# Where the decay tables of a chunked scan are made: inside the forward scan, or ahead of it during the attention and parked in DRAM

## The chip, the cores and the metric

The kernel runs on one core of one Trainium2 chip. The metric is the device time of one execution in microseconds. The kernel before took 2136.37 us, the median of three runs (2135.49 to 2142.13).

## The reference, cut to what matters

Two layers of a hybrid encoder run on 1040 tokens (16 learned ones and 1024) of 1024 channels. Each layer is a norm, one wide projection that is split among four mixers (pooling, a 2-D Fourier transform, a bidirectional scan, attention with eight query heads), their gates, and an output projection with a residual sum. The change is in the scan mixer (SSD):

```python
dt = softplus(dt_raw.reshape(b, n, 2, SSD_HEADS) + dt_bias)
a = -exp(a_log)
...
cs = cumsum(dt * a, axis=-1)                      # within a chunk
seg = cs[..., :, None] - cs[..., None, :]
lmat = exp(where(lower, seg, -inf))
cb = einsum("bclgn,bcsgn->bcgls", cc, bc)
y_diag = einsum("bcgrls,bcsgrp->bclgrp", cb[:, :, :, None] * lmat, x * dt)
decay_to_end = exp(cs[..., -1:] - cs)
chunk_states = einsum("bclgn,bcgrl,bclgrp->bcgrpn", bc, decay_to_end, x * dt)
... # states carried from chunk to chunk
y_off = einsum("bclgn,bcgrpn,bcgrl->bclgrp", cc, prev, exp(cs))
y = y_fwd + y_bwd + d_skip * x
```

For each chunk and head, `lmat` times `dt` is a 104x104 table that depends on `dt` alone and not on the chunk's B, C and x. The forward and the backward direction use two halves of it (a lower and an upper triangle), so the kernel makes both in one table.

## The kernel before, in words

Data lie with channels on partitions. A layer is written as a set of Python generators, each of which issues a few instructions per step. `weave` interleaves several generators in proportion to given step counts, `run` runs them out, and a scheduler then arranges each engine's instructions. So the order around the change is set by step counts (`FN`, `LS`, `PS`, `TT`), by buffer counts (`NBIG` 30 tiles `big`, `NBB` 5 tiles `bb`, `NPF` tiles `pf`) and by the rings of PSUM tiles. Each engine runs its own instructions strictly in that order.

A layer goes through these stages:

- Projections, `mm3`: each product is three matmuls of split operands (L132 to L134). `split` makes the operands on ScalarE (L128) and VectorE (L129).
- Attention in four head pairs, t = 0 to 3. `att_q` and `att_max` prepare the next pair: the row maxima come from scores L626 and the reduction L627 on VectorE, 54 per pair and layer. `att_main` makes the scores again (L655, L656), exponentials on ScalarE (L658) into tiles `pf`, sums of them into `acc` (L666, L668; on GpSimd, six of sixteen on VectorE), the weighted values on PE (L678), and the division. Woven with it runs `fill`, the other projections, which are spilled to DRAM in the order of the string `FO`: U and P (pooling), F (Fourier gate), D (`spill_dt` and `ssd_dt`), C (convolution), R, Z. L621 is a copy within SBUF on GpSimd's DMA queue.
- `ssd_dt` makes from `dt` the running sums `csd`, the decays `ecd` and the token table `tkd`, and writes them to DRAM.
- The Fourier stages (L525 copies a product from PSUM), `ssd_load` (SiLU of the convolved inputs, L306 and the lines behind it on ScalarE), and `ssd_bwd`, the states of the backward direction.
- `ssd_fwd`, the forward scan, in 10 chunks of 104 tokens. `prepare(q)` loads both `csd` rows of a chunk, broadcast over partitions (`rf`, `rb`, two of the five tiles `bb`), and builds the table: the products of C and B in PSUM are masked into `cfb` (L880, L881); for each of eight heads VectorE adds a gap and takes a minimum (L883), ScalarE takes the exponential (L884); ScalarE scales one masked product (L887), VectorE adds the other (L888); GpSimd multiplies the two (L889). `finish(q)` loads `ecd` into a tile `big`, multiplies the contributions of the states from PSUM by it (L900, L903), adds them on GpSimd (L908), carries the state on in `ssd_state` (VectorE L808, PE L811, GpSimd L817, VectorE L818), multiplies the table with x on PE (L914), and adds D times x (L917).
- Woven into the scan, the output projection of the attention. Its group with `pool=True` copies a sum from PSUM on ScalarE (L349), adds the residual on GpSimd (L350) and stores it (L353); it loads into tiles `sms` (L338), of which there are four.

The code of the functions that the change touches:

## Time and profile before

| what | value |
|---|---|
| median of three runs | 2136.37 us |
| profiled execution, time | 2144.23 us |
| its span and mean granted TensorE clock | 2142.5 us, 0.969 |
| TensorE busy | 2007.5 us, 94% |
| VectorE, ScalarE, GpSimd busy | 65%, 47%, 22% |
| forward scans | about 925 to 1050 us and 1981 to 2100 us |
| head pairs of the attention | about 150 to 640 us and, in layer 1, 1205 to 1695 us |

Busy shares are averages over stages that differ, so the windows of single stages carry the argument. A row of a group gives line, engine, operation, output and inputs with their shapes, count, then busy us in all, mean ns of one, and the idle time just before with what ended it. A matmul's duration overlaps with its neighbours', so counts times durations of matmuls aren't added up; a stretch's busy time divided by its count is used for the pace.

### The profile page before, as it was taken

The page shows a single profiled execution, that of the slowest core. Times are in us where ns is not written, and L with a number is a line of the kernel's source. Part 1 is how long each engine was busy: PE and PEld are TensorE (multiplying, and loading weights), DVE is VectorE, ACT ScalarE, POOL GpSimd, SP SyncE. Part 2 cuts the span into 40 slices and gives each one's busy share as a digit, 9 for nine tenths or more (in the row PEclk, how much of TensorE's full clock was granted, in tenths as well). Part 3 has the DMA queues.
Part 4 walks back from the last instruction along what each step waited for, and adds up shares of the span by engine and source line. Part 5 has one row for each costly group of instructions (what it writes and reads, how often), then busy time and mean ns, then how long its engine had stood idle before and what let it go on. Part 6 is the DMA issues. An engine that isn't in the chain of part 4 may idle for free.

```text
span 2142.5 us, 33401 instructions
## 1 busy us (share of the span) xinstructions
PE 2007.5 (94%) x11880; PEld 1756.2 (82%) x11880; DVE 1398.6 (65%) x2785; ACT 1012.6 (47%) x2191; POOL 464.2 (22%) x465
## 2 busy tenths in 40 slices
PE   6999999999999898888889999999999998979888
PEld 5898988688899568877779988877888995878878
DVE  5575547767664455689795655476675635476996
ACT  5534344453542546356464344435534433463652
POOL 2012122031110210245230221221311103012550
PEclk9999999999999999999999999998999999988999
DMA  4322222123233477676643221212223344776666
GB/s 138 99 74 62 64 63 57 43 76 97 91 127 104 135 210 246 193 187 191 169 123 116 66 67 54 73 44 72 68 98 102 117 129 127 241 217 180 175 184 195
DMA packets 164605, 261.01 MB, mean 122 GB/s; under 512 B 20878, under 2 KB 113618, under 8 KB 164438
## 3 DMA queue, kind: packets, MB, share of 16 engines
q1 hardware_dynamic: 161782, 249.55, 38.7%
q0 software_dynamic: 2656, 9.33, 1.8%
q8 instruction: 93, 1.52, 0.3%
q14 instruction: 74, 0.61, 0.1%
HBM read 182.91 MB, written 71.67 MB: 119 GB/s over the span
## 4 chain that ended last, share of the span: by engine, by line
PE 68%; DVE 14%; DMA 9%; ACT 4%; issue 3%; POOL 2%; SPq 1%; DVEq 0%; POOLq 0%; ACTq 0%
PE psmm L132 11%; PE psmm L133 10%; PE psmm L134 10%; PE pspv L678 6%; PE psy L132 5%; PE psy L133 5%; PE psy L134 5%; PE psy L655 2%; PE psy L626 2%; PE psy L656 2%; DMA hd<-sms 2%; DVE bb L883 1%; PE pssc L655 1%; DMA big<-ecd 1%; PE pssc L626 1%
## 5 line engine op out<-in xcount | busy, mean ns | idle before, releaser
L132 PE MATMUL psmm<-big,wh 128*128 128x346 f32 (+2 forms) x1920 | 645.5, 337 | 42.0 <-DVE sms L352 19.2
L133 PE MATMUL psmm<-big,wh 128*128 128x346 f32 (+2 forms) x1920 | 633.8, 330 | 7.6 <-DVE big L129 4.7
L134 PE MATMUL psmm<-big,wl 128*128 128x346 f32 (+2 forms) x1920 | 628.2, 327 | 1.3 <-DVE wl L129 1.3
L132 PEld LDWEIGHTS psmm<-big,wh 128*128 128x128 f32 x1920 | 370.8, 193 | 88.0 <-issue 29.3
L133 PEld LDWEIGHTS psmm<-big,wh 128*128 128x128 f32 x1920 | 371.0, 193 | 17.8 <-DVE big L129 7.2
L134 PEld LDWEIGHTS psmm<-big,wl 128*128 128x128 f32 x1920 | 371.3, 193 | 4.5 <-DVE wl L129 2.4
L668 POOL TENSOR_TENSOR acc<-acc,pf 116x346 f32<-116x346 f32 (+5 forms) x216 | 222.9, 1044 | 701.2 <-ACT pf L658 557.4
L128 ACT CAST wh<-wr 128x512 fp32r<-128x512 f32 (+1 forms) x236 | 145.2, 616 | 268.6 <-PE psmm L133 205.8
L129 DVE TENSOR_TENSOR wl<-wr,wh 128x512 fp32r<-128x512 f32 x232 | 168.4, 730 | 126.6 <-ACT wh L128 125.2
L132 PE MATMUL psy<-big,wh 128*128 128x346 f32 (+2 forms) x672 | 221.8, 330 | 1.1 <-ACT big L128 0.6
L133 PE MATMUL psy<-big,wh 128*128 128x346 f32 (+2 forms) x672 | 217.7, 324 | 3.1 <-DVE big L188 2.0
L134 PE MATMUL psy<-big,wl 128*128 128x346 f32 (+2 forms) x672 | 216.8, 323 | 0.0
L678 PE MATMUL pspv<-pf,vt 116*64 116x346 f32 (+5 forms) x864 | 168.8, 469 | 0.0
L658 ACT ACTIVATE pf<-psy 116x346 f32<-116x346 f32 (+4 forms) x288 | 125.3, 457 | 87.0 <-PE psy L656 84.8
L668 DVE TENSOR_TENSOR acc<-acc,pf 116x346 f32<-116x346 f32 (+5 forms) x120 | 106.7, 889 | 71.5 <-ACT pf L658 51.0
L627 DVE TENSOR_REDUCE mx<-psy 116x1 f32<-116x346 f32 (+3 forms) x272 | 132.7, 511 | 18.5 <-PE psy L626 18.0
L132 PEld LDWEIGHTS psy<-big,wh 128*128 128x128 f32 x672 | 127.2, 189 | 13.3 <-issue 7.6
L133 PEld LDWEIGHTS psy<-big,wh 128*128 128x128 f32 x672 | 127.0, 189 | 6.9 <-DVE big L188 3.1
L134 PEld LDWEIGHTS psy<-big,wl 128*128 128x128 f32 x672 | 127.0, 189 | 0.8
L678 PEld LDWEIGHTS pspv<-pf,vt 116*64 116x64 f32 (+1 forms) x864 | 59.4, 137 | 62.5 <-issue 26.7
L655 PE MATMUL psy<-big,big 128*116 128x346 f32 (+4 forms) x288 | 96.2, 336 | 0.9 <-DVE mx L627 0.8
L627 DVE TENSOR_REDUCE mx<-pssc 128x1 f32<-128x346 f32 (+3 forms) x136 | 69.8, 513 | 41.7 <-PE pssc L626 40.0
(293 smaller groups left out, 3326.7 us busy)
## 6 DMA issues: line engine op xcount, KB each, us to landing
wr<-w SPq DMA_DIRECT2D x248, 256.0 KB
sms<-hd SPq DMA_DIRECT2D x112, 173.0 KB
hd<-sms SPq DMA_DIRECT2D x96, 173.0 KB
bb<-csd SPq DMA_DIRECT2D x40, 338.0 KB
md<-big SPq DMA_DIRECT2D x24, 520.0 KB
gd<-sms SPq DMA_DIRECT2D x64, 173.0 KB
big<-gd SPq DMA_DIRECT2D x16, 520.0 KB
big<-md SPq DMA_DIRECT2D x16, 520.0 KB
```

Of the source, the lines that this page charges most:

```text
L128: nc.scalar.copy(hi, src)
L129: nc.vector.tensor_tensor(lo, src, f(hi), op=ALU.subtract)
L132: nc.tensor.matmul(out_ps, ah, bh, start=start, stop=False)
L133: nc.tensor.matmul(out_ps, ah, bl, start=False, stop=False)
L134: nc.tensor.matmul(out_ps, al, bh, start=False, stop=stop)
L626: nc.tensor.matmul(p[:qn, :cw], s1[e][:, q0:q0 + qn], k1[:, c0:c0 + cw], start=True, stop=True)
L627: nc.vector.tensor_reduce(mx[:qn, q, e, ci:ci + 1], p[:qn, :cw], axis=AX.X, op=ALU.max)
L655: nc.tensor.matmul(p[:n, :cw], k1[:, k0:k0 + n], s1[e][:, cs], start=True, stop=False)
L656: nc.tensor.matmul(p[:n, :cw], k3[0:65, k0:k0 + n], q2[e][0:65, cs], start=False, stop=True)
L658: nc.scalar.activation(pf[:n, :cw], p[:n, :cw], AF.Exp, scale=0.125)
L668: eng.tensor_tensor(accs[c0, e][:n, :cw], accs[c0, e][:n, :cw], pf[:n, :cw], op=ALU.add)
L678: nc.tensor.matmul(hold["pv"][64 * e:64 * e + 64, :cw], s.vt[:n, k, v, :], pfs[e][:n, :cw], start=(k == 0), stop=(k == len(KTS) - 1))
```

## The change

The tables no longer wait for the chunk's B and C. A new generator, `ssd_tab`, makes decay times step size for each of ten chunks and each of two halves (four heads), in six steps per half, and stores the result in DRAM (`dec`). It is woven as one more stream into `att_main` of head pairs 1, 2 and 3, with 40, 44 and 40 steps. It uses a buffer `tb` and a token table `tk`, one of each. In the forward scan, `prepare` loads the finished table of a chunk (one load of 338 KB in the place of two) and multiplies it by the product of C and B from PSUM, two instructions on VectorE. The `ecd` load moves from `finish` to `prepare` and into a tile `bb`. `ssd_state` makes one product on VectorE and one on GpSimd where it made two of half the size. The projection of `dt` and `ssd_dt` go ahead of P and F in `FO`, and `ssd_dt` yields twice more in each of its five rounds. `NPF` goes from 14 to 12; the tiles `cfb` and `gap` are gone. The number of matmuls stays. ScalarE's table loads go from 61 to 57 in its order.

```diff
-    PB, KB, NPF, NACC = 2, 3, 14, 4
+    KB, NPF, NACC = 3, 12, 4
+    TT = (0, 40, 44, 40)
-    FO = 'UPFDCCCCCRCCCZ'
+    FO = 'UDPFCCCCCRCCCZ'
...
             nc.vector.tensor_scalar(t1[R], t1[R], -1.0, None, op0=ALU.mult)
+            yield
+            yield
             p = ps("xx")
...
+    def ssd_tab(l, s):
+        mf, mb = ct[:QC, C_MF:C_MF + QC], ct[:QC, C_MB:C_MB + QC]
+        s.dec = drp.tile([NQ, QC, 8 * QC], F32, name=nm("dec"))
+        for q in range(NQ):
+            tok = phase["p"].tile([QC, 152], F32, name=nm("tk"), tag="tk", bufs=1)
+            nc.sync.dma_start(tok[:, :144], s.tkd[q])
+            for a in range(2):
+                t = phase["p"].tile([QC, 3, 4, QC], F32, name=nm("tb"), tag="tb", bufs=1)
+                rf, rb, cf = t[:, 0], t[:, 1], t[:, 2]
+                col = lambda c, r: tok[:, c + 4 * a + r:c + 4 * a + r + 1]
+                nc.sync.dma_start(t[:, 0:2], s.csd[q, :, 4 * a:4 * a + 4].partition_broadcast(QC))
+                yield
+                for r in range(4):
+                    nc.scalar.activation(cf[:, r], mb, AF.Copy, scale=col(136, r))
+                if a == 0:
+                    nc.vector.tensor_tensor(tok[:, 144:152], tok[:, 32:40], tok[:, 0:8], op=ALU.subtract)
+                yield
+                for r in range(4):
+                    nc.vector.scalar_tensor_tensor(cf[:, r], mf, col(104, r), cf[:, r], op0=ALU.mult, op1=ALU.add)
+                gap = tok[:, 144 + 4 * a:148 + 4 * a].unsqueeze(2).broadcast_to([QC, 4, QC])
+                nc.gpsimd.tensor_tensor(rb, rb, gap, op=ALU.add)
+                yield
+                nc.vector.tensor_tensor(rf, rf, rb, op=ALU.min)
+                yield
+                for r in range(4):
+                    nc.scalar.activation(rf[:, r], rf[:, r], AF.Exp, bias=col(0, r))
+                yield
+                nc.gpsimd.tensor_tensor(rf, rf, cf, op=ALU.mult)
+                nc.gpsimd.dma_start(s.dec[q, :, 4 * a * QC:4 * a * QC + 4 * QC], rf)
+                yield
...
+        nc.vector.tensor_tensor(hv(xw), hv(x[:QC]), w.unsqueeze(3).broadcast_to([QC, 4, 2, 64]), op=ALU.mult)
...
+            nc.gpsimd.tensor_tensor(hv(new), hv(st), d.unsqueeze(3).broadcast_to([128, 4, 2, 64]), op=ALU.mult)
...
         def prepare(q):
-            rf, rb = vr(bb()[:QC]), vr(bb()[:QC])
-            nc.sync.dma_start(rf, s.csd[q, 0].partition_broadcast(QC))
-            nc.sync.dma_start(rb, s.csd[q, 1].partition_broadcast(QC))
+            rb, e = vr(bb()[:QC]), vr(bb())
+            nc.sync.dma_start(rb, s.dec[q].rearrange("s (r t) -> s r t", t=QC))
+            for a in range(2):
+                nc.sync.dma_start(e[64 * a:64 * a + 64].rearrange("p (i j) t -> p i j t", i=2), s.ecd[q, :, 4 * a:4 * a + 4].partition_broadcast(64))
...
-            nc.vector.tensor_tensor(cf, pcv, mf.unsqueeze(1).broadcast_to([QC, 2, QC]), op=ALU.mult)
-            nc.vector.tensor_tensor(cb, pcv, mb.unsqueeze(1).broadcast_to([QC, 2, QC]), op=ALU.mult)
-            for r in range(8):
-                nc.vector.scalar_tensor_tensor(rf[:, r], rb[:, r], s.gap[:, q, r:r + 1], rf[:, r], op0=ALU.add, op1=ALU.min)
-                nc.scalar.activation(rf[:, r], rf[:, r], AF.Exp, bias=tok[:, r:r + 1])
-            for r in range(8):
-                g = (r % 4) // 2
-                nc.scalar.activation(rb[:, r], cb[:, g], AF.Copy, scale=tok[:, 136 + r:137 + r])
-                nc.vector.scalar_tensor_tensor(rb[:, r], cf[:, g], tok[:, 104 + r:105 + r], rb[:, r], op0=ALU.mult, op1=ALU.add)
-            nc.gpsimd.tensor_tensor(rb, rb, rf, op=ALU.mult)
+            for a in range(2):
+                m = rb[:, 4 * a:4 * a + 4].rearrange("p (g i) t -> p g i t", g=2)
+                nc.vector.tensor_tensor(m, m, pcv, op=ALU.mult)
...
-        run(weave((att_main(l, s, t), LS + 3 * PC), (chain(*side), 20 + 3 * PC + 6), (islice(fill, n), n)))
+        run(weave((att_main(l, s, t), LS + 3 * PC), (chain(*side), 20 + 3 * PC + 6), (islice(fill, n), n), (islice(tab, TT[t]), TT[t] + 0.01)))
...
-        run(weave((islice(main, LS + 3 * PC - 1), LS + 3 * PC - 1), (chain(*side), PS), (chain(fill, islice(fill2, GP + FB[0])), WF * (n + GP + FB[0]))))
+        run(weave((islice(main, LS + 3 * PC - 1), LS + 3 * PC - 1), (chain(*side), PS), (chain(fill, islice(fill2, GP + FB[0])), WF * (n + GP + FB[0])), (tab, TT[3])))
```

In the kernel after, `ssd_tab` has these lines: loads L786 and L791, copies L794 and exponentials L806 on ScalarE, L799 and the minimum L803 on VectorE, the addition L801, the product L808 and the store L809 on GpSimd. The lines of before's attention stand one further there (L627 is L628, L668 is L669). In the scan the new products are L910; L900 and L903 have become L918 and L921.

What the order of each engine shows. On GpSimd, in head pair 1 of layer 0 before, there are only sums of exponentials:

```order
L666 TENSOR_TENSOR acc_1767<-pf_1734,pf_1760 116x346
L668 TENSOR_TENSOR acc_1767<-acc_1767,pf_1800 116x346
L668 TENSOR_TENSOR acc_1767<-acc_1767,pf_1853 116x346
L668 TENSOR_TENSOR acc_1769<-acc_1769,pf_1858 116x346
L668 TENSOR_TENSOR acc_1767<-acc_1767,pf_1880 116x346
L668 TENSOR_TENSOR acc_1767<-acc_1767,pf_1917 116x346
```

After, additions, products and stores of the tables stand between such sums; this is from head pair 2:

```order
L801 TENSOR_TENSOR tb_4517<-tb_4517,tk_4273 104x416
L669 TENSOR_TENSOR acc_2924<-acc_2924,pf_2994 116x348
L669 TENSOR_TENSOR acc_2926<-acc_2926,pf_2999 116x348
L669 TENSOR_TENSOR acc_2924<-acc_2924,pf_3025 116x348
L808 TENSOR_TENSOR tb_4517<-tb_4517 104x416
L809 DMA dec_2882<-tb_4517 104x416
L669 TENSOR_TENSOR acc_2924<-acc_2924,pf_3078 116x348
L801 TENSOR_TENSOR tb_4704<-tb_4704,tk_4702 104x416
```

A sum that stands behind an addition or a product of a table cannot start before it.

On VectorE, in the same stage before, row maxima of the next head pair are what stands between the sums and the splits:

```order
L627 TENSOR_REDUCE mx_2118<-pssc_2660 116x1
L627 TENSOR_REDUCE mx_2118<-psy_2663 116x1
L627 TENSOR_REDUCE mx_2118<-psy_2666 116x1
L668 TENSOR_TENSOR acc_2116<-acc_2116,pf_2677 116x346
L668 TENSOR_TENSOR acc_2116<-acc_2116,pf_2695 112x346
L627 TENSOR_REDUCE mx_2118<-psy_2708 116x1
L627 TENSOR_REDUCE mx_2118<-psy_2711 116x1
L627 TENSOR_REDUCE mx_2118<-pssc_2714 116x1
```

After, a minimum stands ahead of six maxima, and four scaled sums and the next minimum behind them:

```order
L803 TENSOR_TENSOR tb_3361<-tb_3361 104x416
L628 TENSOR_REDUCE mx_2183<-pssc_2430 116x1
L628 TENSOR_REDUCE mx_2183<-psy_2433 116x1
L628 TENSOR_REDUCE mx_2183<-psy_2436 116x1
L628 TENSOR_REDUCE mx_2183<-pssc_2458 116x1
L628 TENSOR_REDUCE mx_2183<-psy_2461 116x1
L628 TENSOR_REDUCE mx_2183<-psy_2464 116x1
L130 TENSOR_TENSOR wl_2514<-wr_2507,wh_2513 128x512
L633 TENSOR_REDUCE mneg_2822<-mx_2183 116x9
L799 SCALAR_TENSOR_TENSOR tb_3594<-ct,tk_3359,tb_3594 104x104 x4
L130 TENSOR_TENSOR wl_2756<-wr_2751,wh_2755 128x512
L803 TENSOR_TENSOR tb_3594<-tb_3594 104x416
```

In a layer the first minimum stands behind the 57th row maximum, the 19th behind the 148th, the last behind the 162nd.

On VectorE in the middle of the forward scan of layer 0, before:

```order
L883 SCALAR_TENSOR_TENSOR bb_9652<-bb_9653,gap_8183,bb_9652 104x104 x3
L880 TENSOR_TENSOR cfb_9496<-psy_9493,ct 104x208
L881 TENSOR_TENSOR cfb_9496<-psy_9493,ct 104x208
L883 SCALAR_TENSOR_TENSOR bb_9652<-bb_9653,gap_8183,bb_9652 104x104 x3
L888 SCALAR_TENSOR_TENSOR bb_9478<-cfb_9496,big_8184,bb_9478 104x104 x4
L883 SCALAR_TENSOR_TENSOR bb_9652<-bb_9653,gap_8183,bb_9652 104x104
L888 SCALAR_TENSOR_TENSOR bb_9478<-cfb_9496,big_8184,bb_9478 104x104 x4
L883 SCALAR_TENSOR_TENSOR bb_9652<-bb_9653,gap_8183,bb_9652 104x104
L808 TENSOR_TENSOR big_9491<-big_9491,big_8184 104x4x64 x2
L129 TENSOR_TENSOR wl_10100<-wr_10097,wh_10099 128x512
L900 TENSOR_TENSOR big_9557<-pssc_9560,big_9557 128x416
L903 TENSOR_TENSOR big_9557<-pspv_9566,big_9557 128x416
```

After, with a chunk's table loaded ready, two products by the PSUM tile take the place of these 18 instructions:

```order
L842 TENSOR_TENSOR big_10012<-big_10012,big_8576 104x512
L910 TENSOR_TENSOR bb_9997<-bb_9997,psxx_10014 104x416 x2
L130 TENSOR_TENSOR wl_10511<-wr_10508,wh_10510 128x512
L918 TENSOR_TENSOR bb_9840<-pssc_10057,bb_9840 128x416
L921 TENSOR_TENSOR bb_9840<-pspv_10063,bb_9840 128x416
```

The products of `ssd_state` (L808 before, L842 after) are one instruction, and L918 and L921 follow without the chain of small instructions ahead of them.

More of the change, by code (lines that the diff above doesn't have):

```diff
@@ L108, in chunk_tile @@
     def chunk_tile(tag, dt=F32):
-        return phase["p"].tile([128, 348], dt, name=nm(tag), tag=tag, bufs=NPF if tag == "pf" else PB)
+        return phase["p"].tile([128, 348], dt, name=nm(tag), tag=tag, bufs=NPF)
     def bb():
@@ L806, in ssd_state @@
         w = s.tok[q][:, 64 + 32 * i:72 + 32 * i].rearrange("p (a j) -> p j a", j=4)
-        for a in range(2):
-            nc.vector.tensor_tensor(hv(xw)[:, :, a], hv(x[:QC])[:, :, a], w[:, :, a].unsqueeze(2).broadcast_to([QC, 4, 64]), op=ALU.mult)
+        nc.vector.tensor_tensor(hv(xw), hv(x[:QC]), w.unsqueeze(3).broadcast_to([QC, 4, 2, 64]), op=ALU.mult)
         p = ps(tag)
@@ L815, in ssd_state @@
             d = s.decb[:, i, :, q].rearrange("p (a j) -> p j a", j=4)
-            for a in range(2):
-                nc.gpsimd.tensor_tensor(hv(new)[:, :, a], hv(st)[:, :, a], d[:, :, a].unsqueeze(2).broadcast_to([128, 4, 64]), op=ALU.mult)
+            nc.gpsimd.tensor_tensor(hv(new), hv(st), d.unsqueeze(3).broadcast_to([128, 4, 2, 64]), op=ALU.mult)
             nc.vector.tensor_tensor(new, new, p, op=ALU.add)
@@ L831, in ssd_load @@
         s.tok = []
-        s.gap = phase["p"].tile([QC, NQ, 8], F32, name=nm("gap"), tag="gap", bufs=1)
         for q0 in (0, 5):
@@ L836, in ssd_load @@
             s.tok += [t[:, i] for i in range(5)]
-            nc.vector.tensor_tensor(s.gap[:, q0:q0 + 5], t[:, :, 32:40], t[:, :, 0:8], op=ALU.subtract)
         s.xbc = [big() for _ in range(8)]
@@ L858, in ssd_fwd @@
         s.y = [s.xbc[j] for j in range(4)]
-        mf, mb = ct[:QC, C_MF:C_MF + QC], ct[:QC, C_MB:C_MB + QC]
         vr = lambda t: t[:, :8 * QC].rearrange("p (r t) -> p r t", t=QC)
@@ L876, in prepare @@
                 nc.tensor.matmul(pc[:QC, g * QC:(g + 1) * QC], s.xbc[4 + g][:, qs], s.xbc[6 + g][:, qs], start=True, stop=True)
-            cfb = phase["p"].tile([128, 4 * QC], F32, name=nm("cfb"), tag="cfb", bufs=1)[:QC].rearrange("p (g t) -> p g t", t=QC)
-            cf, cb = cfb[:, 0:2], cfb[:, 2:4]
-            pcv = pc[:QC, :2 * QC].rearrange("p (g t) -> p g t", t=QC)
-            nc.vector.tensor_tensor(cf, pcv, mf.unsqueeze(1).broadcast_to([QC, 2, QC]), op=ALU.mult)
-            nc.vector.tensor_tensor(cb, pcv, mb.unsqueeze(1).broadcast_to([QC, 2, QC]), op=ALU.mult)
-            for r in range(8):
-                nc.vector.scalar_tensor_tensor(rf[:, r], rb[:, r], s.gap[:, q, r:r + 1], rf[:, r], op0=ALU.add, op1=ALU.min)
-                nc.scalar.activation(rf[:, r], rf[:, r], AF.Exp, bias=tok[:, r:r + 1])
-            for r in range(8):
-                g = (r % 4) // 2
-                nc.scalar.activation(rb[:, r], cb[:, g], AF.Copy, scale=tok[:, 136 + r:137 + r])
-                nc.vector.scalar_tensor_tensor(rb[:, r], cf[:, g], tok[:, 104 + r:105 + r], rb[:, r], op0=ALU.mult, op1=ALU.add)
-            nc.gpsimd.tensor_tensor(rb, rb, rf, op=ALU.mult)
-            ready[q] = (xt, xw, bt, rb)
+            pcv = pc[:QC, :2 * QC].rearrange("p (g t) -> p g t", t=QC).unsqueeze(2).broadcast_to([QC, 2, 2, QC])
+            for a in range(2):
+                m = rb[:, 4 * a:4 * a + 4].rearrange("p (g i) t -> p g i t", g=2)
+                nc.vector.tensor_tensor(m, m, pcv, op=ALU.mult)
+            ready[q] = (xt, xw, bt, rb, e)
         def finish(q, st):
             qs = slice(q * QC, (q + 1) * QC)
-            xt, xw, bt, rb = ready.pop(q)
-            e = vr(big())
-            for a in range(2):
-                nc.sync.dma_start(e[64 * a:64 * a + 64].rearrange("p (i j) t -> p i j t", i=2), s.ecd[q, :, 4 * a:4 * a + 4].partition_broadcast(64))
+            xt, xw, bt, rb, e = ready.pop(q)
             if q < NQ - 1:
@@ L1034, in hybrid_trunk @@
         s.md["x"] = drp.tile([8, 128, L], F32, name=nm("md"))
-        kv = att_kv(l, s)
+        kv, tab = att_kv(l, s), ssd_tab(l, s)
         if l == 0:
```

1 line of the change is left out of this document (removed).

## The prediction

> **What bounds the kernel now.** I read the page first (busy time, chain), then the windows of busy time by stage, then groups, waits and timelines in the two stages touched. Line numbers are those of the kernel before unless "new" stands ahead.
>
> ```profile
> PE 2007.5 (94%) x11880; PEld 1756.2 (82%) x11880; DVE 1398.6 (65%) x2785; ACT 1012.6 (47%) x2191; POOL 464.2 (22%) x465
> PE 68%; DVE 14%; DMA 9%; ACT 4%; issue 3%; POOL 2%; SPq 1%; DVEq 0%; POOLq 0%; ACTq 0%
> ```
>
> TensorE bounds the program as a whole. That average hides two kinds of stage. The windows are, in this order: layer 0's head pairs 0 to 1, the stretch with the dt tables, the run-up to the forward scan, the scan; then layer 1's stretch with the dt tables, its run-up and its scan (columns: length, busy us of PE, PEld, DVE, ACT, POOL, granted clock, DMA share, GB/s).
>
> ```profile
> 150.00:355.00 205.00, 204.31 (x1240) 178.18 (x1238) 110.06 (x194) 94.72 (x210) 53.11 (x57) 1.00 0.21 64
> 355.00:425.00 70.00, 65.38 (x336) 49.15 (x333) 54.36 (x148) 29.63 (x69) 8.26 (x8) 0.98 0.13 38
> 820.00:925.00 105.00, 88.75 (x556) 81.81 (x555) 70.93 (x162) 54.12 (x112) 18.17 (x21) 0.95 0.72 207
> 925.00:1050.00 125.00, 109.16 (x729) 100.37 (x729) 113.85 (x256) 70.49 (x190) 59.62 (x53) 0.95 0.68 186
> 1400.00:1470.00 70.00, 67.69 (x306) 47.53 (x302) 56.77 (x153) 23.60 (x64) 11.42 (x12) 0.85 0.11 27
> 1876.00:1981.00 105.00, 91.01 (x536) 83.63 (x538) 70.00 (x160) 51.94 (x109) 18.03 (x21) 0.89 0.69 198
> 1981.00:2100.00 119.00, 103.83 (x711) 95.77 (x706) 110.93 (x256) 69.81 (x189) 62.03 (x53) 0.94 0.66 181
> ```
>
> In the attention PE is full and nothing else is: VectorE 54%, ScalarE 46%, GpSimd 26%. In the scan VectorE is 91 to 93% busy and PE is not. There 125 − 109.2 = 15.8 us (layer 1: 119 − 103.8 = 15.2) are PE idle, and the clock missing from 1.00 is worth 0.05 × 125 = 6.3 (0.06 × 119 = 7.1). So about 22 us per layer is all that the scan can give before PE itself is the bound. The waits of the scan (us in total, times, longest) name who holds it:
>
> ```profile
> PE pspv L811 <- DVE big L903: 10.9, 6, 3.7
> PE psmm L132 <- ACT sms L349: 4.1, 4, 2.1
> SPq L353 <- POOL sms L350: 45.5, 20, 5.6
> ```
>
> The first is VectorE's queue; the other two are the ring of `sms` buffers of the woven output projection, which the change does not touch.
>
> The profiled execution took 2144.2 us, 7.9 over the median of 2136.4. The clock of 0.85 in layer 1's dt stretch against 0.98 in layer 0's, 0.13 × 70 = 9 us, is about that. I therefore set the change against the median; against the profiled execution it is the same difference.
>
> **Part by part: what leaves the scan.**
>
> ```profile
> L883 DVE SCALAR_TENSOR_TENSOR bb<-bb,gap,bb 104x104 f32<-104x104 f32 x160 | 64.5, 453 | 5.5 <-DMA bb<-csd 5.4
> L884 ACT ACTIVATE bb<-bb,big 104x104 f32<-104x104 f32 x160 | 50.7, 377 | 36.5 <-DVE bb L883 30.3 <-issue 5.8
> L888 DVE SCALAR_TENSOR_TENSOR bb<-cfb,big,bb 104x104 f32<-104x104 f32 x160 | 48.8, 362 | 1.2 <-ACT bb L887 1.2
> L887 ACT ACTIVATE bb<-cfb,big 104x104 f32<-104x104 f32 x160 | 46.0, 370 | 11.7 <-DVE cfb L881 11.4
> L889 POOL TENSOR_TENSOR bb<-bb,bb 104x832 f32<-104x832 f32 x20 | 41.8, 2089 | 60.8 <-DVE bb L888 60.8
> L900 DVE TENSOR_TENSOR big<-pssc,big 128x416 f32<-128x416 f32 x18 | 10.5, 584 | 6.3 <-DMA big<-ecd 4.9 <-issue 1.4
> L908 POOL TENSOR_TENSOR big<-big 128x416 f32<-128x416 f32 x16 | 18.6, 1161 | 13.5 <-DVE big L903 13.5
> L880 DVE TENSOR_TENSOR cfb<-psy,ct x12: 359/362/370, 898.5 to 2086.4; 104x208 f32<-104x208 f32 x12
> ```
>
> Per layer VectorE loses (64.5 + 48.8)/2 = 56.7 us and 20 mask products of 0.36 (L880, and L881 like it), 7.2: 63.9 in all. It gains two products from PSUM per chunk, new L910, of the shape of L900: 20 × 0.58 = 11.7. Net −52 of 114, so VectorE falls to about half of the stage. ScalarE loses (50.7 + 46.0)/2 = 48, GpSimd 21. The two merged products of ssd_state, one read of the same elements instead of two halves, I count at nothing here, since VectorE no longer sets the end. Two loads of 338 KB per chunk become one, and the `ecd` load goes from finish to prepare, earlier and in the ring of five `bb`; that takes a load off SP's queue right where SP waits for L350, and I count nothing for it.
>
> Of the 22 us I take two thirds, 15 per layer, 30 in all. The third that stays is the `sms` ring (4.1 us of PE wait in layer 0) and the serial step from state to L903, which no longer stands behind other VectorE work but is still there. Bounds: 22 if PE closes up wholly; 0 if ring and transfers hold the scan anyway (rival C).
>
> In the run-up ScalarE changes tables for a first few exponentials of the scan between two groups of SiLU:
>
> ```profile
> 828.23 1.28 ACT L306 ACT_TABLE_LOAD   x1 [0.52 <-DMA big<-md]
> 832.54 1.28 ACT L884 ACT_TABLE_LOAD   x1
> 834.23 1.28 ACT L306 ACT_TABLE_LOAD   x1
> PE psy L132 <- ACT big L525: 4.1, 1, 4.1
> ```
>
> The second and third loads fall away, 2.6 us, together with exponentials and copies that interleave with L525, for which PE waits 4.1. I take 3 per layer, 6 in all (0 to 4 each).
>
> **What comes into the attention.** Per layer ScalarE takes on 160 operations of 0.37 = 60 us, VectorE 80 × 0.36 + 20 × 0.58 = 41, GpSimd 40 × 1.16 = 46 and 20 DMA issues. Each stays within the idle time of the windows above, and as ScalarE's table is the exponential's there anyway (L658), no table load comes with it. As work it is therefore hidden. Its cost is in its order: the buffer `tb` exists once, so a half chunk is one serial chain from its load to its store, and each link stands at a fixed place in an engine's queue. If a link is late, what stands behind it is late too: behind the minimum (new L803) the row maxima, behind the GpSimd pair (new L801, L808) the accumulators, behind the exponentials (new L806) those of the scores, and behind those PE.
>
> ```profile
> L668 POOL TENSOR_TENSOR acc<-acc,pf x216: 890/935/2032, 151.8 to 1807.8; 116x346 f32<-116x346 f32 x64, 116x348 f32<-116x348 f32 x16, 116x332 f32<-116x332 f32 x16, 112x346 f32<-112x346 f32 x8
> L668 DVE TENSOR_TENSOR acc<-acc,pf x120: 443/993/1257, 152.2 to 1809.2; 116x346 f32<-116x346 f32 x64, 116x348 f32<-116x348 f32 x16, 112x346 f32<-112x346 f32 x16, 116x332 f32<-116x332 f32 x16
> L627 DVE TENSOR_REDUCE mx<-psy x68: 500/507/522, 213.8 to 395.2; 116x1 f32<-116x346 f32 x46, 116x1 f32<-116x348 f32 x22
> DMA to landing us min/median/max: 2.9/3.3/4.5
> 858.42 2.35 DMA sms<-md
> 954.41 4.29 DMA bb<-csd
> ```
>
> The chain T of one half: add 1.16 and product 1.16 (L908's row), minimum 0.58 (L900's), four exponentials 1.5, store 3.3 (the landing row, of L621, the only DMA on GpSimd's queue), load between 2.35 and 4.29, taken at 3.3: 11.0 us. For queueing behind half an operation at four hand-overs I add 0.3: T = 11.3. Low, with 2.9 and 2.35: 9.7. High, with 4.5 and 4.29: 13.2.
>
> The place that it has: by the order, the first minimum of a layer stands behind the 57th row maximum and the 19th behind the 148th. Those two ran at 213.8 and 395.2 before (first and last of the L627 row): 181 us for 18 intervals. Since the dt tables have moved out of this stretch, 125 more matmuls stand in it (939 before, 1064 now, counted in the order), at 204.3/1240 = 0.165 us each 20 us, and 70 − 65.4 = 5 us of idle PE leave it: (181 + 20 − 5)/18 = 10.9 us. So the chain lags 0.4 us per half, over 36 intervals of both layers 14 us. With T = 10.9 or less it is 0. Each 1 us above costs 36.
>
> Moving the dt projection ahead shifts VectorE's crowded 70 us from head pair 1 to pair 0, ten fill steps longer: I count nothing (the 5 us idle per layer leave one place and may come back in the other, −5 to +5). Two fewer `pf` buffers leave twelve, two batches of six: nothing, as ScalarE's L658 waits for scores and not for buffers; up to a few us if it does, within the range.
>
> **A rule that speaks against it.** The trace shows VectorE and GpSimd in each other's way where both read SBUF:
>
> ```profile
> 964.64 0.32 DVE L883 SCALAR_TENSOR_TENSOR bb<-bb,gap,bb 104x104 f32<-104x104 f32 x1
> 965.59 0.58 DVE L900 TENSOR_TENSOR big<-pssc,big 128x416 f32<-128x416 f32 x1
> 966.59 2.73 DVE L883 SCALAR_TENSOR_TENSOR bb<-bb,gap,bb 104x104 f32<-104x104 f32 x3
> 965.75 1.95 POOL L889 TENSOR_TENSOR bb<-bb,bb 104x832 f32<-104x832 f32 x1 [1.15 <-DVE bb L888]
> 967.65 1.07 POOL L908 TENSOR_TENSOR big<-big 128x416 f32<-128x416 f32 x1
> ```
>
> Beside GpSimd's products three L883 took 2.73 us, where one just before took 0.32, while L900, with one operand in PSUM, kept its 0.58; the accumulators on VectorE, 0.44 at the least, take 0.99 at the median. The Trainium skill, page "SBUF — State Buffer", section "SBUF: two separate sides", states the cause as a lock: a VectorE operation with two SBUF inputs and a GpSimd operation exclude each other for the whole instruction. The trace agrees. By that rule the minimum, both inputs in SBUF, may wait for a whole GpSimd operation, which by the L668 row is 0.9 us: T = 12.2. [...]
>
> **The sum.** −30 − 6 + 14 = −22: 2136.4 − 22 = 2114 (against the profiled execution 2122).
>
> **Rivals.**
> B, slower: the tab chain paces the attention. At new L803 VectorE holds the row maxima back. It decides from the point where 36 us of gain are spent over 36 intervals, 10.9 + 1.0 = 11.9 us per half. With the lock, T = 12.2: 36 × 1.3 − 36 = +11, 2147; with the slow ends of the transfers, T = 13.2: +47, 2183. For: one buffer, two DMAs in each half, four engines in one chain. Against: the four copies and four STTs are off it, and low DMA share in the attention (0.21). Chance 0.26, of which 0.10 for the far end.
> C, no change: the scan does not shorten, since SP's 45.5 us behind L350 and the `sms` ring hold the woven projection as before, and transfers are busy 0.68; the gain of VectorE is idle time. Then the run-up's 6 and a little of the scan go against 14: about 2136. Against: the largest PE wait is VectorE's. Chance 0.14.
> D, all of it: 44 from the scans and 6 from the run-ups, T under 10.9: 2136 − 50 = 2086. Chance 0.10.
> A, the forecast, 2114, for T between 10.9 and 11.7 and a scan gain of 12 to 22 per layer: own range 2095 to 2130. Chance 0.50.
>
> **How the numbers follow.** About 0.3%, 6.4 us, is what a measurement of this kernel can tell: faster is below 2130, slower above 2142.8. Faster: A and D, 0.60. Same: C, 0.14. Slower: B, 0.26. The range reaches from 2092 to 2158: it leaves out D's lower part and B's far end, under 0.2 in all.
>
> **What would show it.** Right: in the scan VectorE about half busy, PE's wait on L903 (new L921) down to a few us, both scans 12 to 20 us shorter; no exponential's table load among the SiLUs; in the attention the distance between two minima near 11 us, and PE idle a few us per head pair, ended by VectorE behind a minimum or by ScalarE behind an exponential. Wrong: minima over 12 us apart and PE idle before the scores (B); scans as long as before, waits on L349/L350 grown (C); attention as long as before with minima 10 us apart (D).

## The result, and the profile after

The kernel after takes 2202.25 us (median of four runs, 2198.15 to 2210.21), the kernel before 2135.93 in the same runs: the ratio is 1.0304, interval 1.0275 to 1.0333. It is slower by 66 us, where 22 us less were forecast. Its profiled execution has a span of 2202.6 us.

The page after, busy time by engine:

```profile
PE 2019.8 (92%) x11880; PEld 1767.1 (80%) x11880; DVE 1389.6 (63%) x2645; ACT 998.5 (45%) x2187; POOL 515.6 (23%) x533
```

PE has the same work and 48 us more idle time in the span. To see where, I cut both kernels at the same events: row maxima of the attention and the first and last product of a table in the scan. These windows of the kernel before are layer 0's row maxima 1 to 55, 55 to 109 and 109 to 163, its scan, and layer 1's scan:

```profile
115.10:213.50 98.40, 97.46 (x597) 87.76 (x595) 66.50 (x124) 42.26 (x96) 22.04 (x25) 1.00 0.20 62
213.50:351.60 138.10, 137.94 (x840) 121.55 (x840) 72.21 (x134) 59.30 (x129) 30.20 (x32) 1.00 0.21 65
351.60:500.40 148.80, 143.96 (x803) 115.66 (x801) 110.82 (x238) 74.73 (x167) 34.91 (x34) 0.99 0.21 66
915.30:1051.70 136.40, 119.35 (x823) 109.01 (x823) 123.62 (x277) 73.74 (x197) 63.10 (x57) 0.95 0.68 186
1973.30:2106.20 132.90, 117.73 (x824) 108.52 (x825) 119.36 (x274) 72.58 (x195) 63.79 (x56) 0.95 0.66 180
```

The same windows of the kernel after:

```profile
114.00:210.00 96.00, 88.32 (x494) 73.50 (x493) 80.90 (x186) 44.15 (x116) 22.88 (x24) 0.95 0.18 50
210.00:390.80 180.80, 158.96 (x868) 134.75 (x866) 115.26 (x230) 94.32 (x252) 68.38 (x75) 0.92 0.34 98
390.80:540.20 149.40, 141.23 (x814) 121.44 (x812) 96.46 (x184) 74.77 (x176) 48.59 (x51) 0.96 0.26 82
969.40:1092.80 123.40, 114.40 (x826) 105.45 (x826) 81.44 (x156) 43.08 (x86) 42.49 (x41) 0.99 0.65 184
2046.50:2167.70 121.20, 111.03 (x827) 103.52 (x828) 81.14 (x156) 42.76 (x86) 42.02 (x41) 1.00 0.66 186
```

The scans went nearly as forecast: 13.0 and 11.7 us shorter, where 15 each were taken, the clock back at 0.99 and 1.00. VectorE is busy for two thirds of them, where about half was forecast. The waits of the scan after (979 to 1102 us), PE's and then SP's, answer to those before:

```profile
PE psmm L133 <- ACT sms L350: 6.4, 4, 3.7
PE pspv L845 <- DVE bb L921: 0.2, 1, 0.2
```

```profile
SPq L354 <- POOL sms L351: 45.3, 20, 4.1
```

The wait on VectorE (before L903) is down from 10.9 to 0.2 us; what is left is the `sms` ring, as the sum had it. The loss is mainly in the second window, head pairs 0 and 1: 42.7 us longer with 28 matmuls more, PE idle 21.8 us where it was 0.2, and the clock at 0.92 where it was 1.00, another 14.5. In layer 1 the same window is 33.5 us longer. Even the first window, before the first minimum of a table, has 103 matmuls less and is only 2.4 us shorter: there the dt tables crowd VectorE (84% busy) and PE is idle 7.7 us.

### The profile page after: what moved, and what is told of

Its sections match the earlier page's. It is cut to its first block, busy times and chain, and to the rows that moved or that the text cites. A ratio compares the mean times of both kernels' runs of the same rounds, so it can differ in the third digit from the quotient of the medians.

```text
span 2202.6 us, 33431 instructions
## 1 busy us (share of the span) xinstructions
PE 2019.8 (92%) x11880; PEld 1767.1 (80%) x11880; DVE 1389.6 (63%) x2645; ACT 998.5 (45%) x2187; POOL 515.6 (23%) x533
## 5 line engine op out<-in xcount | busy, mean ns | idle before, releaser
L133 PE MATMUL psmm<-big,wh 128*128 128x346 f32 (+2 forms) x1904 | 636.8, 335 | 34.7 <-ACT sms L350 12.3
L134 PE MATMUL psmm<-big,wh 128*128 128x346 f32 (+2 forms) x1904 | 625.3, 328 | 9.4 <-DVE big L130 6.5
L135 PE MATMUL psmm<-big,wl 128*128 128x346 f32 (+2 forms) x1904 | 621.5, 327 | 0.0
L133 PEld LDWEIGHTS psmm<-big,wh 128*128 128x128 f32 x1904 | 365.2, 192 | 78.3 <-issue 26.1
L134 PEld LDWEIGHTS psmm<-big,wh 128*128 128x128 f32 x1904 | 365.2, 192 | 19.3 <-DVE big L130 10.5
L669 POOL TENSOR_TENSOR acc<-acc,pf 116x346 f32<-116x346 f32 (+5 forms) x216 | 224.6, 1051 | 541.0 <-ACT pf L659 493.8
L130 DVE TENSOR_TENSOR wl<-wr,wh 128x512 fp32r<-128x512 f32 x232 | 172.5, 748 | 139.1 <-ACT wh L129 134.4
L133 PE MATMUL psy<-big,wh 128*128 128x346 f32 (+2 forms) x688 | 231.7, 337 | 16.1 <-DVE sms L353 15.9
L134 PE MATMUL psy<-big,wh 128*128 128x346 f32 (+2 forms) x688 | 228.7, 332 | 3.2 <-DVE big L189 1.7
L135 PE MATMUL psy<-big,wl 128*128 128x346 f32 (+2 forms) x688 | 227.5, 331 | 0.1
L679 PE MATMUL pspv<-pf,vt 116*64 116x346 f32 (+5 forms) x864 | 161.8, 480 | 0.0
L133 PEld LDWEIGHTS psy<-big,wh 128*128 128x128 f32 x688 | 134.6, 196 | 28.5 <-DVE sms L353 16.5
L628 DVE TENSOR_REDUCE mx<-psy 116x1 f32<-116x346 f32 (+3 forms) x272 | 132.8, 511 | 30.7 <-PE psy L627 30.4
L134 PEld LDWEIGHTS psy<-big,wh 128*128 128x128 f32 x688 | 134.8, 196 | 8.4 <-DVE big L189 3.5
L669 DVE TENSOR_TENSOR acc<-acc,pf 116x346 f32<-116x346 f32 (+5 forms) x120 | 96.6, 805 | 63.0 <-ACT pf L659 56.7
L135 PEld LDWEIGHTS psy<-big,wl 128*128 128x128 f32 x688 | 135.0, 196 | 1.3 <-DVE wl L130 0.4
L353 DVE TENSOR_TENSOR sms<-sms,psmm 128x346 f32<-128x346 f32 (+2 forms) x104 | 52.7, 510 | 74.7 <-PE psmm L135 42.4
```

The lines of the kernel that those rows point to most:

```text
L130: nc.vector.tensor_tensor(lo, src, f(hi), op=ALU.subtract)
L133: nc.tensor.matmul(out_ps, ah, bh, start=start, stop=False)
L134: nc.tensor.matmul(out_ps, ah, bl, start=False, stop=False)
L135: nc.tensor.matmul(out_ps, al, bh, start=False, stop=stop)
L353: nc.vector.tensor_tensor(o, ht, p[:, :cw], op=ALU.add)
L628: nc.vector.tensor_reduce(mx[:qn, q, e, ci:ci + 1], p[:qn, :cw], axis=AX.X, op=ALU.max)
```

## The experiments

Two theories stood at the start. **Lag**: the serial chain of a half chunk takes longer than the place that the order gives it. **Work**: the tables' operations, GpSimd's above all, slow the attention wherever they stand. Each ratio compares with runs of the kernel before on the same chip, whose median lay between 2134 and 2137 us. Differences between two experiments are taken between their medians, in part across chips; those of under about 5 us mean little.

### The parts by themselves

The tables left out:

```diff
-            nc.sync.dma_start(rb, s.dec[q].rearrange("s (r t) -> s r t", t=QC))
+            nc.sync.dma_start(rb, s.csd[q, 0].partition_broadcast(QC))
-        ..., (islice(tab, TT[t]), TT[t] + 0.01)))
+        ...))
```

> The kernel after without the making of the tables in the attention; the scan loads one broadcast row of running sums of the same 338 KB in the place of the finished table, so what the tables are worth is left out and the rest of the change stays (the scan's shorter work, the dt tables moved ahead). Both theories, lag and work, give the gain of the scans as the profile after has it, about 39 us, less what moving the dt tables costs. If that move costs nothing: 2097. If it costs what PE loses in the first stretch of pair 0 (7.6 us idle and 0.10 x 72 = 7.2 of clock in layer 0, near 15 per layer, less the 9 to 11 that the same tables cost in head pair 1 before): about 2107. Over 2115 would say that the attention loses time in another way than by the tables.

Measured 2109.6 (ratio 0.987, 0.985 to 0.989). So the tables cost 2202 − 2110 = 93 us in the attention.

The dt projection and its tables moved, in the kernel before:

```diff
-    FO = 'UPFDCCCCCRCCCZ'
+    FO = 'UDPFCCCCCRCCCZ'
+            yield
+            yield
             p = ps("xx")
```

> The kernel before with nothing changed but the place of the dt projection and its tables (ahead of P and F, and the two further steps per round). If the crowding on VectorE only changes its place, as the prediction had it: 2136, same. If pair 0 pays about 15 us per layer and pair 1 gets back about 10: 2146. If nothing comes back: 2166.

Measured 2154.4 (1.009, 1.006 to 1.011): the move alone costs 17 us against the kernel before on this chip (2137.2), 18 against the median of 2136. With the move in place, the rest of the change is worth 2154.4 − 2109.6 = 45 us: by the windows of these two runs 11.1 and 14.5 in the scans and 2.9 and 7.1 in the run-ups, 35.6 in all; the other 9 are spread over the rest. The three parts, −45 + 18 + 93 = +66, must add up, since each is the difference of two neighbouring runs; that each would be worth the same without the others is not shown.

### Order and work

Each of the tables' instructions is issued behind the attention's latest one on its engine:

```diff
+        def behind(e):
+            return tc.issue_after(latest[e])
...
+                with behind("v"):
                     nc.vector.tensor_tensor(rf, rf, rb, op=ALU.min)
```

> The kernel after with the same instructions and the same single buffer, but each of the tables' instructions is issued behind the latest score exponential or accumulation of its own engine, so that the order follows the program: 20 half chunks are spread over head pairs 1 to 3, about 20 us each, where the order of the kernel after put them 10 us apart. Theory lag (the serial chain of 13 us is longer than the place that the order gives it, and every engine waits at its next link): the cost in the attention is nearly gone, 2105 to 2135. Theory work (the tables' 60 us of ScalarE, 41 of VectorE, 46 of GpSimd per layer and the mutual blocking of VectorE and GpSimd slow the attention wherever they stand): as the kernel after, 2185 to 2205.

Measured 2170.2 (1.015, 1.013 to 1.017). Spreading saves 32 of 93 us, between what the two theories had.

Operations alone on constants, without chain, loads and stores, with step counts `TT` of 40, 79, 1 and 1, which put them into the stretch of attention where the kernel after has them (the edit for GpSimd's product; the others alike):

```diff
-                nc.gpsimd.tensor_tensor(rf, rf, cf, op=ALU.mult)
-                nc.gpsimd.dma_start(s.dec[q, :, 4 * a * QC:4 * a * QC + 4 * QC], rf)
+            with behind("p"):
+                nc.gpsimd.tensor_tensor(z, wide, z, op=ALU.mult)
```

> The tables' operations alone: as many of the same shapes on the same engines in head pairs 0 and 1, where the kernel after has them (minima behind the 54th to the 162nd row maximum), but each engine works on a plane of its own, from constants, and waits for no other; their loads and stores are left out, and the scan loads a row of running sums in place of the table. Theory lag: within 10 us of the kernel that leaves the tables out altogether. Theory work: most of the 99 us that the attention lost stays, 2170 to 2200.

Measured 2150.2 (1.006, 1.004 to 1.007): 41 us over the kernel without tables. So the prediction's "as work it is hidden" fails for 41 us, and 52 need chain, loads, stores or the tighter order of the kernel after. Which operations? First without GpSimd's two:

```diff
-            with behind("p"):
-                nc.gpsimd.tensor_tensor(z, wide, ct[:QC, 0:4].unsqueeze(2).broadcast_to([QC, 4, QC]), op=ALU.add)
...
-            with behind("p"):
-                nc.gpsimd.tensor_tensor(z, wide, z, op=ALU.mult)
```

> The kernel with the tables' operations alone (2150), without its two GpSimd operations per half; like it, it leaves out the tables, their loads and stores. If GpSimd and the blocking between it and VectorE make the 40 us that the operations cost: 2110 to 2118. If ScalarE's and VectorE's queues make them (each score waits for an exponential that stands behind four copies): 2140 to 2150.

Measured 2113.8 (0.989, 0.987 to 0.991): ScalarE's 60 and VectorE's 41 us per layer cost 4 us. They are hidden. Then the counterpart:

```diff
-                for r in range(4):
-                    nc.scalar.activation(x[:, r], mb, AF.Copy, scale=col)
...
-                nc.vector.tensor_tensor(y, y, wide, op=ALU.min)
```

> The counterpart: only the two GpSimd operations per half are left of the tables' work. By the blocking: 2130 to 2150. By the queues of ScalarE and VectorE: 2110 to 2118.

Measured 2129.9 (0.997, 0.995 to 0.999): GpSimd's two operations cost 20 by themselves, and 36 beside the others (2150.2 − 2113.8).

The chain shortened by the store's landing:

```diff
-                nc.gpsimd.tensor_tensor(rf, rf, cf, op=ALU.mult)
-                nc.gpsimd.dma_start(s.dec[q, :, 4 * a * QC:4 * a * QC + 4 * QC], rf)
+                nc.gpsimd.tensor_tensor(cf, rf, cf, op=ALU.mult)
+                nc.gpsimd.dma_start(s.dec[q, :, 4 * a * QC:4 * a * QC + 4 * QC], cf)
```

> The kernel after, but the tile of a half chunk is two tiles: the product is written into the plane of the scaled masks and stored from there, so that the next load waits for the product and not for the landing of the store. That takes the store's 0.3 + 0.6 + 2.0 us out of the serial chain, floor 7.5 in place of 10.1. The order puts the minima closer in answer (the 19th of a layer behind the 126th row maximum, not the 148th). If it is the length of the chain that counts, 36 x 2.6 = 94 of at most 52 are won: the cost falls to that of the work alone, 2150. If it is the gap between what the order allows and what the chain takes, the place shrinks with the chain and 2180 to 2205 stays.

Measured 2210.5 (1.034, 1.031 to 1.037). A shorter chain gains nothing. It is what lag gives with a shrinking place: the order puts the 19th minimum of layer 0 behind the 126th row maximum, and the minima stand 11.7 us apart where they stood 13.0.

The paced kernel with dt in its old place, the tables in pairs 2 and 3:

```diff
-    TT = (0, 40, 44, 40)
+    TT = (0, 0, 60, 60)
-    FO = 'UDPFCCCCCRCCCZ'
+    FO = 'UPFDCCCCCRCCCZ'
-            yield
-            yield
             p = ps("xx")
```

> The paced kernel with the dt tables back in their old place and step count, the tables made in head pairs 2 and 3, some 17 us per half chunk. The scans' gain without the move is 2136 - (2110 - 18) = 44; the work costs 40 if it costs the same there, the chain nothing at that pace: 2132. If the end of pair 3, where products of the Fourier stage wait for splits on ScalarE, pays 15 per layer as in the paced kernel: 2150 to 2165.

Measured 2196.8 (1.028, 1.025 to 1.030), a miss: 32 to 65 us over what was expected. In this trace the stretch from the 109th to the 163rd row maximum of layer 0 takes 164.5 us for 802 matmuls (before: 148.8 for 803), and the one that ends at the backward scan 316.4 (294.7): the dt tables, pair 3 and the preparation of the Fourier stage have less room for tables than pair 1. The two causes were not separated here.

### GpSimd out of the chain

```diff
-                nc.gpsimd.tensor_tensor(rb, rb, gap, op=ALU.add)
-                yield
-                nc.vector.tensor_tensor(rf, rf, rb, op=ALU.min)
+                yield
+                for r in range(4):
+                    nc.vector.scalar_tensor_tensor(rf[:, r], rb[:, r], col(144, r), rf[:, r], op0=ALU.add, op1=ALU.min)
...
-                nc.gpsimd.tensor_tensor(rf, rf, cf, op=ALU.mult)
-                nc.gpsimd.dma_start(s.dec[...], rf)
+                nc.vector.tensor_tensor(rf, rf, cf, op=ALU.mult)
+                nc.sync.dma_start(s.dec[...], rf)
```

> The kernel after with the tables made without GpSimd: the gap and the minimum in one VectorE instruction per head, as the scan had them, the product on VectorE, the store on SP's queue. The order is the scheduler's, minima still 10 to 11 us apart. If the GpSimd operations make the cost, by their own time and by the blocking: work 4, and the chain without two hand-overs, 2115 to 2140. If what makes the other 52 us is that the order is tighter than the chain, whatever the chain consists of: 2160 to 2175.

Measured 2129.0 (0.997, 0.995 to 0.998). The tables cost 19 us in place of 93, in the scheduler's own order. From load to load a half takes 11.9 us at the median here and 12.4 in the kernel after (13.1 and 14.0 at the mean, over 38 intervals), hardly less. That does not refute lag, since this order is wider, 12 us per half and not 10 to 11 as expected: the 19th minimum of layer 0 stands behind the 162nd row maximum, not the 148th. The table at the end of the next part sets place and distance of the halves side by side.

The same, paced (one of the operations is shown):

```diff
-    TT = (0, 40, 44, 40)
+    TT = (0, 62, 57, 1)
...
+                with behind("v"):
                     nc.vector.tensor_tensor(rf, rf, cf, op=ALU.mult)
```

> The same tables without GpSimd, and each instruction issued behind the latest score exponential or accumulation of its engine, the 20 halves in head pairs 1 and 2, some 13 to 15 us apart. If order and work are the two causes, both are gone: 2110 + 4 + a few, 2114 to 2125, faster than the kernel before. If the chain costs something of its own wherever it stands: 2140 or more.

Measured 2124.9 (0.995, 0.993 to 0.998), 15 over the kernel without tables. Pacing gains 4 us at most once GpSimd is out.

```diff
-    FO = 'UDPFCCCCCRCCCZ'
+    FO = 'UPDFCCCCCRCCCZ'
```

> The kernel of the run before with the dt projection behind P (U, P, D, F), so that its tables fall at the end of head pair 0 and not at its start, beside the row maxima of two pairs. If the 18 us of the move come from the place at the start of pair 0: 8 to 18 us less than the run before. If any earlier place costs the same, within 4 us of it.

Measured 2143.1 (1.004, 1.002 to 1.005), the opposite of the hope: 18 more. The later place is worse.

The paced kernel of above, GpSimd in it, with other step counts:

```diff
-    TT = (0, 40, 44, 40)
+    TT = (0, 62, 57, 1)
```

> The tables with GpSimd as in the change, paced over pairs 1 and 2 like the two runs before. Against the paced kernel of three pairs (2170) the 16 us per layer that pair 3 lost are saved. Work 40 and no lag: 2150. If GpSimd's operations cost only where the chain waits for them: 2115 to 2130.

Measured 2163.7 (1.013, 1.010 to 1.016), above both expected values: with GpSimd, paced, 39 over the same without it. These two kernels have the same step counts and nearly the same order, 13.4 to 13.7 us per half, so here it is the three steps on GpSimd that make the 39. Against the kernel after, which has the same steps on GpSimd, the wider order saves another 39.

One piece at a time (in these three the store is on SP's queue; the second takes the addition off GpSimd as above, the third the product):

```diff
-                nc.gpsimd.dma_start(s.dec[q, :, 4 * a * QC:4 * a * QC + 4 * QC], rf)
+                nc.sync.dma_start(s.dec[q, :, 4 * a * QC:4 * a * QC + 4 * QC], rf)
```

> The kernel after with only the store of a half moved from GpSimd's queue to SP's. If the store's issue on GpSimd (0.57 us, 40 times, and the accumulations behind it) matters: 2165 to 2190. If the two arithmetic operations do it: 2195 to 2205.

Measured 2168.8 (1.013, 1.009 to 1.016): the store alone is 33 of the 93 us, and the minima stand at the same places of the order as in the kernel after.

> The store on SP's queue and the addition fused into VectorE's minimum; the product stays on GpSimd. If addition and product share the cost, half of the 73 us less than with the store alone moved: 2160 to 2170. If the addition, which waits for the load with the accumulations behind it, makes it all: 2125 to 2140.

Measured 2141.5 (1.002, 0.9995 to 1.004): another 27.

```diff
-                nc.gpsimd.tensor_tensor(rf, rf, cf, op=ALU.mult)
+                nc.vector.tensor_tensor(rf, rf, cf, op=ALU.mult)
```

> The store on SP's queue and the product on VectorE; the addition stays on GpSimd. Half and half: 2160 to 2170. If the addition makes it all: 2185 to 2200. If the product makes it all: 2125 to 2140.

Measured 2147.9 (1.004, 1.003 to 1.006): 21 with the product in place of the addition. Both together gave 40 (2168.8 − 2129.0), about their sum of 48, and about the 36 that the same two cost as mere work. In these runs the order is wider too, as the table below shows.

Tables without GpSimd, `FO`, `TT` and the steps of `ssd_dt` as in the paced late kernel, the order the scheduler's:

```diff
-    TT = (0, 40, 44, 40)
+    TT = (0, 0, 60, 60)
-    FO = 'UDPFCCCCCRCCCZ'
+    FO = 'UPFDCCCCCRCCCZ'
```

> Tables without GpSimd, and the dt projection in its old place, the tables in head pairs 2 and 3. If tables and move add up: 2129 - 18 = 2111. If the tables meet the crowded stretch of the dt tables and the end of pair 3, as the paced late kernel with GpSimd did: 2130 to 2150.

Measured 2131.4 (0.996, 0.994 to 0.998). Tables and move don't add up. The stretch from the 109th to the 163rd row maximum of layer 0, where the tables now meet the dt tables, takes 156.0 us, against 139.1 in the run without GpSimd that has the dt tables ahead.

### Who stands behind GpSimd

Open was why GpSimd matters so much with the halves about as far apart as ever. In the attention, GpSimd's own work are sums of exponentials (L668, after L669). If those stand behind its waits, taking them away should free it:

```diff
-                eng = nc.vector if e == 1 and k % 3 else nc.gpsimd
+                eng = nc.vector
```

> The kernel without the tables (2110; the scan again loads running sums in their place, so the tables are left out) with the attention's sums of exponentials all on VectorE and none on GpSimd: the base for the next run. VectorE takes on 216 sums of 0.5 us alone, 108 us, and is blocked no more: 2110 to 2140.

Measured 2079.1 (0.975, 0.973 to 0.976), a surprise: without tables, this alone is 31 us faster than the kernel with the sums shared out (2109.6); the two ran on different chips, and by the ratios it is 27.

The same edit in the kernel after:

> The kernel after with the sums all on VectorE: GpSimd has nothing left in the attention but the tables' two operations and store, and can wait without anybody behind it. If the queue is the cause: the tables cost 15 to 40 over the run before, in place of 93. If the blocking of VectorE's operations and the chain are: 60 or more.

Measured 2123.3 (0.996, 0.994 to 0.997): the tables, with GpSimd's three steps in them, now cost 44 us, not 93. A half still takes 12.0 us at the median. That fits sums held up behind the tables' waits, but the order has changed as well (the table below). In the waits of GpSimd from 205 to 500 us, the kernel without tables shows a queue that waits for its own work, the exponentials:

```profile
POOL acc L669 <- ACT pf L659: 122.4, 30, 35.4
```

the kernel after one that stands at the tables' links, and whose slack has gone:

```profile
POOL tb L801 <- DMA tb<-csd: 79.7, 15, 7.3
POOL acc L669 <- ACT pf L659: 38.4, 19, 4.6
POOL tb L808 <- ACT tb L806: 30.4, 10, 9.4
POOL tb L808 <- DVE mx L628: 11.4, 5, 3.9
POOL dec L809 <- POOL tb L808: 5.6, 19, 0.3
```

and the kernel with the sums on VectorE one that waits even longer, with nobody behind:

```profile
POOL tb L801 <- DMA tb<-csd: 93.1, 17, 6.5
POOL tb L801 <- DVE tk L796: 66.7, 2, 57.5
POOL tb L808 <- ACT tb L806: 62.9, 15, 10.4
POOL tb L808 <- DVE mx L628: 14.1, 4, 8.3
```

One round on GpSimd in the kernel after (start, us, operation, idle before) shows how the 10.5 us between two additions go by with one sum in them:

```profile
340.44 0.88 POOL L801 TENSOR_TENSOR tb<-tb,tk 104x416 f32<-104x416 f32 x1 [4.59 <-DMA tb<-csd]
343.25 1.06 POOL L808 TENSOR_TENSOR tb<-tb 104x416 f32<-104x416 f32 x1 [1.94 <-ACT tb L806]
344.61 0.56 POOL L809 DMA_DIRECT2D dec<-tb  x1 [0.30 <-POOL tb L808]
345.66 0.93 POOL L667 TENSOR_TENSOR acc<-pf,pf 116x346 f32<-116x346 f32 x1 [0.49 <-ACT pf L659]
350.99 0.88 POOL L801 TENSOR_TENSOR tb<-tb,tk 104x416 f32<-104x416 f32 x1 [4.40 <-DMA tb<-csd]
```

It is busy 3.4 of 10.5 us and stands at a link for most of the rest. ScalarE is held in the same way; its waits from 205 to 500 us in the kernel after:

```profile
ACT tb L806 <- DVE tb L803: 46.0, 15, 5.9
ACT tb L794 <- DMA dec<-tb: 30.8, 13, 3.9
```

And PE, in the same stretch, waits for scores' exponentials and for row maxima, in pieces of up to 3 us. Both stand in queues between the tables' operations. In the run without tables the first of these rows reads 4.2 us, and there is no wait for a row maximum:

```profile
PE pssc L627 <- ACT pf L659: 5.3, 2, 3.1
PE psy L656 <- ACT pf L659: 5.2, 4, 2.8
PE pssc L656 <- DVE mx L628: 2.7, 3, 2.3
PE pssc L627 <- DVE mx L628: 2.3, 3, 1.4
```

The other part is the blocking, which the prediction weighed. These rows of the sums on VectorE (min/median/max ns) are of the kernel without tables and with shared sums:

```profile
L669 DVE TENSOR_TENSOR acc<-acc,pf x120: 488/998/1253, 149.9 to 1801.6; 116x346 f32<-116x346 f32 x64, 116x348 f32<-116x348 f32 x16, 112x346 f32<-112x346 f32 x16, 116x332 f32<-116x332 f32 x16
```

and with all sums on VectorE:

```profile
L669 DVE TENSOR_TENSOR acc<-acc,pf x336: 491/511/524, 150.4 to 1764.9; 116x346 f32<-116x346 f32 x96, 116x348 f32<-116x348 f32 x24, 116x332 f32<-116x332 f32 x24, 112x346 f32<-112x346 f32 x16
```

Beside GpSimd's sums a VectorE sum takes twice its time at the median; without them none is over 0.524 us. The tables' minimum after, and the row maxima, whose input is in PSUM:

```profile
L803 DVE TENSOR_TENSOR tb<-tb x40: 567/592/3074, 214.1 to 1563.9; 104x416 f32<-104x416 f32 x40
L628 DVE TENSOR_REDUCE mx<-psy x272: 495/508/522, 114.2 to 1675.3; 116x1 f32<-116x348 f32 x49, 128x1 f32<-128x348 f32 x41, 116x1 f32<-116x346 f32 x23, 128x1 f32<-128x346 f32 x23
```

Ten of the 40 minima are held, by 0.7 to 2.5 us, each while a GpSimd operation runs; 85 of the 408 maxima run beside one, and none is held. That is what the Trainium skill, page "SBUF — State Buffer", section "SBUF: two separate sides", states: an operation of VectorE and one of GpSimd exclude each other only if the first has two SBUF inputs and the second reads SBUF, or if the first runs in a two-port mode.

How much room did each order give? I took the VectorE instructions around the first and the 19th minimum of a layer and looked when the same instructions run in the kernel without tables (for the sums on VectorE, in the one without tables that also has them there). The time between them over 18 is the place of a half. Beside it stands the distance at which the minima ran (us, layer 0 / layer 1), and what the tables cost:

| kernel | place | distance | cost |
|---|---|---|---|
| after | 10.4 / 11.4 | 13.0 / 13.5 | 93 |
| product in a tile aside | 9.1 / 9.1 | 11.7 / 11.8 | 101 |
| store on SP | 10.4 / 11.4 | 12.2 / 13.1 | 59 |
| store on SP, product on VectorE | 11.5 / 12.1 | 12.5 / 13.3 | 38 |
| store on SP, addition on VectorE | 11.2 / 11.5 | 12.3 / 12.2 | 32 |
| without GpSimd | 12.1 / 12.0 | 12.8 / 12.5 | 19 |
| sums on VectorE | 11.9 / 11.6 | 13.1 / 12.6 | 44 |
| paced over two pairs | 13.5 / 13.4 | 15.3 / 15.0 | 54 |
| the same without GpSimd | 13.7 / 13.5 | 14.2 / 14.2 | 15 |

Distance less place, times 18 for each layer, is within 9 us of the cost in every row (84 us for the kernel after): the time is lost where the halves stand. Why is another question. All edits that take arithmetic or sums off GpSimd in the scheduler's order have also widened the place, so lag and the queue are not fully separated. Three comparisons hold the place nearly still, and each relieves GpSimd and saves time: the store on SP (33 us), the paced pair (39 us), and layer 1 with the sums on VectorE, where the 18 intervals together lose 18 us against their place and not 38, at a place of 11.6 us against 11.4.

## Why the prediction was wrong, step by step

**Scan and run-up: right.** Forecast 36 us, measured 45 by the difference of two runs, of which 35.6 are in the scans and run-ups. In the kernel after, the scans give 13.0 + 11.7 us and the run-ups 0.5 + 7.7 (of the 7.7 us, 6.8 are the clock, 0.90 before and 1.00 after in a window of 67.8 us); the exponential's table load among the SiLUs is gone.

**"In the attention as work it is therefore hidden": wrong for GpSimd.** This is the step that failed, and with it the price of the tables: +14 us in the sum, 93 measured. ScalarE's and VectorE's operations cost 4 us, as argued. GpSimd's two, 39 us a layer in the trace (46 forecast) on an engine 26% busy, cost 20 us by themselves and 36 beside the others; its three steps cost 39 where the halves had room. The share of busy time did not show it: GpSimd was idle because its sums wait for exponentials. That the sums need this slack to catch up is argued from the wait rows and not shown by itself. The rest of the 93 comes with the tight order and the waits in it; how much of that is lag and how much the sums behind GpSimd's waits stays open.

**T, the chain against its place: too small by about 2 us per half.** T was taken at 11.3 us and the place at 10.9. In layer 0 the first and the 19th minimum stand 233.8 us apart, 13.0 per half; in layer 1 it is 13.5. The place was also read too wide: 213.8 and 395.2 are the times of the 55th and the 156th row maximum. The 57th and the 148th ran at 214.6 and 388.8, 174 us apart, which by the prediction's own sum gives 10.5, and 190/18 = 10.6 in the run without tables. (In layer 1 a head pair has 48 row maxima and not 54; there the place is 11.4.) So the lag is 2.6 and 2.1 us per half where 0.4 was taken. By "each 1 us above costs 36" that is some 85 us, near the 93 measured. But T is not a property of the chain alone, as the sum had it: with the same place, the store off GpSimd's queue shortens the distance by 0.8 and 0.4 us, and at a place of 13.4 to 13.7 us the minima still stand 1.6 to 1.8 us further apart than that with GpSimd, and 0.5 to 0.7 without.

**Rival B, slower, named the lock and the queue,** and what it would show, minima over 12 us apart with PE idle before the scores, is what the trace shows (12.2 at the median). Yet it priced the lock only by what it adds to T (0.9 us, 2147), and its far end, slow transfers, at 2183. The store landed faster than taken (2.3 us at the median, not 3.3); the row used for it is of L621, which is not the only DMA on that queue, as the Fourier tables' loads (L496, L502) are on it too.

**Moving the dt tables at nothing, −5 to +5: wrong, 17 to 18.** The range was too narrow because I took the cost of the crowd to move with it. In layer 0, in the first window after it costs 7.7 us idle and 4.8 of clock; in its old place the window from the 109th to the 163rd maximum lost 4.8 and 1.5. The run with D behind P shows that still another place costs 18 more.

**The clock** was left out of the attention's cost. In the window of 180.8 us, 21.8 us of idle PE come with 14.5 us of clock below 1.00. Waits of a few us are therefore priced too low if only the idle time is counted.
